# Two groups of operand sums behind the last plain column of three feed-forwards

## The chip, the cores and the metric

The kernel runs on one core of one Trainium2 chip, as one program. The metric is the device time of one execution in microseconds (us), the median over several runs. The engines named below are TensorE (PE, with its weight loads as PEld), VectorE (DVE), ScalarE (ACT), GpSimd (POOL) and SyncE (SP, which issues the loads of weights). Each engine goes through its own list of instructions in the order in which the program was laid out, and waits at an instruction until what it needs is there.

## The reference

An encoder trunk of two layers over 512 tokens of width 1024, in float32. Each layer has a feed-forward, a mixer, a second feed-forward and a gated embedding, so there are four feed-forwards in all.

```python
def swiglu(x, w_gu, w_down):
    g, u = jnp.split(x @ w_gu, 2, axis=-1)        # D_FF = 2816
    return (jax.nn.silu(g) * u) @ w_down

for i in range(DEPTH):                            # DEPTH = 2
    h = h + 0.5 * swiglu(rmsnorm(h, ffn1_norm[i]), ffn1_w_gu[i], ffn1_w_down[i])
    hn = rmsnorm(h, mix_norm[i])
    h = h + (ssd_mixer if i % 2 == 0 else neighbourhood_attention)(hn, ...)
    h = h + 0.5 * swiglu(rmsnorm(h, ffn2_norm[i]), ffn2_w_gu[i], ffn2_w_down[i])
    gate = jax.nn.sigmoid(rmsnorm(h, ple_norm[i]) @ ple_w_gate[i])
    h = h + gate * rmsnorm(p[i] @ ple_w_proj[i], ple_post_norm[i])
```

## The kernel before

Tokens lie along the free dimension (512 of them), features along the 128 partitions; `h` is eight tiles of 128x512. A product in float32 is made of three rounded ones: an operand is cut into a rounded part ("hi", or `wh` for weights) and the rest ("lo", `wl`), and `gemm` issues hi times hi (L298), hi times lo (L301) and lo times hi (L302) for each 128 rows of the inner dimension. ScalarE makes the rounded part of a weight tile (L231) and VectorE the rest (L233). There are three tiles of each, so the fourth weight can be cut only when the products with the first are through.

The 22 column blocks of a feed-forward's gate and up matrices are handled in two ways. The first ones are "plain": a gate product of 24 matmuls, an up product of 24 matmuls, then `activate` (L474 gate times the norm's factor, L475 silu, L477 and L478 the up half, L327 and L328 the cut into hi and lo). The others go two at a time through a scheme with seven smaller products per pair of columns (`block`, L539), which needs sums and differences of the residual's tiles. These are made once per feed-forward, in four groups, by `sums(kk)` for kk = 0 to 3: two scaled tiles (L498), differences (L501, L502, L520, L521) and their cuts (L507, L508, L327, L328, L524, L525). A group has 12 instructions on VectorE and six on ScalarE. It also may cut one weight tile ahead of its own work (`prep_next`).

The first feed-forward has six plain columns (`FIRST`), the other three have four (`OTHERS`, columns 0 to 3). In these three, the group 0 is called in column 1, the group 1 ahead of column 2, the group 2 ahead of column 3 and the group 3 behind column 3. After the plain columns come two "pairs" of down products: output tiles 0 and 1, then 2 and 3, each with four columns' results as the inner dimension, 12 matmuls per tile, 48 in all (called d0 to d3 below, each with its weight tile). Then the blocks begin.

`issue_after`, the tile pools and a list scheduler fix the order per engine: an instruction called earlier stands earlier unless the scheduler's own estimate has its input coming late. So where a call stands decides the place of its instructions on VectorE and ScalarE, and with them that of the weight cuts next to them. TensorE's list follows too: where the estimate has a weight late, products that come later in the program may be drawn ahead of it.

## Time and profile before

| | |
|---|---|
| median of 3 runs | 2274.69 us (2274.47 to 2274.8) |
| profiled execution | 2274.88 us |
| its span, first to last instruction | 2273.0 us |
| granted TensorE clock, mean | 0.999 |
| TensorE busy | 2265.7 us |
| VectorE busy | 1823.0 us |
| ScalarE busy | 1284.3 us |

The span is what the trace covers; the execution's time is 1.9 us longer. In a row of the timeline the first number is the start in us from the span's beginning, the second how long the row lasted; a row with x2 holds two instructions. A 128x512 matmul is listed with 0.39 us, but one starts every 0.227 us, because the next begins while the last results drain: the distance between starts shows whether TensorE waited. On VectorE too the listed time is longer than the distance between starts (0.68 us listed, 0.60 us from start to start for 128x512).

The last plain column and the pairs lie at 923 to 940 us in the second feed-forward, at 1322 to 1341 us in the third and at 1907 to 1924 us in the fourth.

### The profile page before, as it was taken

The page shows a single profiled execution, that of the slowest core. Times are in us where ns is not written, and L with a number is a line of the kernel's source. Part 1 is how long each engine was busy: PE and PEld are TensorE (multiplying, and loading weights), DVE is VectorE, ACT ScalarE, POOL GpSimd, SP SyncE. Part 2 cuts the span into 40 slices and gives each one's busy share as a digit, 9 for nine tenths or more (in the row PEclk, how much of TensorE's full clock was granted, in tenths as well). Part 3 has the DMA queues.
Part 4 walks back from the last instruction along what each step waited for, and adds up shares of the span by engine and source line. Part 5 has one row for each costly group of instructions (what it writes and reads, how often), then busy time and mean ns, then how long its engine had stood idle before and what let it go on. Part 6 is the DMA issues. An engine that isn't in the chain of part 4 may idle for free.

```text
span 2273.0 us, 33245 instructions
## 1 busy us (share of the span) xinstructions
PE 2265.7 (100%) x12458; PEld 1948.5 (86%) x12458; DVE 1823.0 (80%) x2711; ACT 1284.3 (57%) x2335; POOL 327.9 (14%) x261
## 2 busy tenths in 40 slices
PE   9999999999999999999999999999999999999999
PEld 7888888888888888888888888888888888988887
DVE  8788878988888958988885898888668758888866
ACT  6444445777677765544457555444557655544563
POOL 0000001345555651000003100000110010000020
PEclk9999999999999999999999999999999999999999
DMA  5323324444444643322323332332557732333232
GB/s 198 114 77 107 107 78 140 162 154 140 146 141 143 208 146 120 116 98 85 102 89 115 108 102 88 98 107 78 173 176 228 227 117 92 103 107 107 79 102 75
DMA packets 105089, 281.56 MB, mean 124 GB/s; under 512 B 13008, under 2 KB 13904, under 8 KB 104928
## 3 DMA queue, kind: packets, MB, share of 16 engines
q1 hardware_dynamic: 104640, 279.30, 37.8%
q8 instruction: 98, 1.61, 0.3%
q14 instruction: 63, 0.52, 0.1%
q10 hardware_dynamic: 288, 0.14, 0.0%
HBM read 259.70 MB, written 13.40 MB: 120 GB/s over the span
## 4 chain that ended last, share of the span: by engine, by line
PE 96%; DVE 3%; ACT 1%; issue 0%; DMA 0%; POOL 0%; SPq 0%; DVEq 0%; POOLq 0%
PE ps L539 31%; PE ps L298 19%; PE ps L302 19%; PE ps L301 19%; PE ps L1023 1%; PE ps L982 1%; PE ps L1377 1%; PE ps L1003 1%; PE ps L1431 1%; PE ps L938 1%; PE ps L927 1%; PE ps L1420 1%; DVE wl L233 0%; DVE md L328 0%; PE ps L1411 0%
## 5 line engine op out<-in xcount | busy, mean ns | idle before, releaser
L298 PE MATMUL ps<-md,wh 128*128 128x512 f32 (+1 forms) x2032 | 796.0, 392 | 0.9 <-ACT md L327 0.9
L302 PE MATMUL ps<-md,wl 128*128 128x512 f32 (+1 forms) x2032 | 790.5, 389 | 0.2 <-DVE wl L233 0.2
L301 PE MATMUL ps<-md,wh 128*128 128x512 f32 (+1 forms) x2032 | 790.1, 389 | 0.0
L231 ACT CAST wh<-wr 128x1024 fp32r<-128x1024 f32 (+2 forms) x395 | 351.7, 892 | 417.4 <-PE ps L301 200.3
L233 DVE TENSOR_TENSOR wl<-wr,wh 128x1024 fp32r<-128x1024 f32 (+2 forms) x395 | 417.6, 1058 | 97.4 <-ACT wh L231 91.6
L302 PEld LDWEIGHTS ps<-md,wl 128*128 128x128 f32 x2032 | 381.5, 188 | 82.3 <-DVE wl L233 1.5
L298 PEld LDWEIGHTS ps<-md,wh 128*128 128x128 f32 x2032 | 381.6, 188 | 77.8 <-ACT md L327 1.4
L301 PEld LDWEIGHTS ps<-md,wh 128*128 128x128 f32 x2032 | 382.0, 188 | 74.0 <-DVE md L598 0.5
L539 PE MATMUL ps<-md,wh 128*128 128x256 f32 (+1 forms) x1610 | 367.2, 308 | 0.0
L539 PE MATMUL ps<-sc,wh 128*128 128x512 f32 (+1 forms) x1190 | 362.3, 357 | 0.0
L364 POOL TENSOR_TENSOR sq<-sq,sq 128x512 f32<-128x512 f32 x71 | 100.9, 1422 | 1612.1 <-ACT sq L360 1261.7
L233 DVE TENSOR_TENSOR wl<-md,wh 128x1024 fp32r<-128x1024 f32 x175 | 214.0, 1223 | 113.6 <-ACT wh L231 112.8
L231 ACT CAST wh<-md 128x1024 fp32r<-128x1024 f32 x175 | 183.8, 1051 | 200.9 <-PE ps L539 129.0
L539 PEld LDWEIGHTS ps<-md,wh 128*128 128x128 f32 x1610 | 263.7, 190 | 20.3
L539 PE MATMUL ps<-md,wl 128*128 128x256 f32 x980 | 276.4, 282 | 0.0
L539 PE MATMUL ps<-sc,wl 128*128 128x256 f32 x980 | 275.7, 281 | 0.0
L539 PEld LDWEIGHTS ps<-sc,wh 128*128 128x128 f32 x1190 | 210.0, 188 | 34.6
L539 PEld LDWEIGHTS ps<-sc,wl 128*128 128x128 f32 x980 | 185.2, 189 | 3.2
L539 PEld LDWEIGHTS ps<-md,wl 128*128 128x128 f32 x980 | 186.1, 190 | 0.0
L827 DVE SCALAR_TENSOR_TENSOR t<-ps,ccw,t 128x510 f32<-128x510 f32 (+1 forms) x180 | 133.3, 743 | 10.5 <-ACT t L820 7.9
L629 DVE SCALAR_TENSOR_TENSOR hs<-ps,hs 128x512 f32<-128x512 f32 x144 | 98.7, 685 | 49.9 <-PE ps L302 49.6
L565 DVE TENSOR_TENSOR t<-ps,t 128x256 f32<-128x256 f32 x280 | 113.4, 417 | 14.0 <-ACT t L562 12.8
(214 smaller groups left out, 2446.4 us busy)
## 6 DMA issues: line engine op xcount, KB each, us to landing
wr<-in_w_gw_dram SPq DMA_DIRECT2D x70, 512.0 KB, 3.3
md<-in_w_gw_dram SPq DMA_DIRECT2D x70, 512.0 KB, 4.5
wr<-in_w_in_dram SPq DMA_DIRECT2D x65, 512.0 KB, 3.2
wr<-in_w_dn_dram SPq DMA_DIRECT2D x128, 256.0 KB, 2.6
wr<-in_w_gu_dram SPq DMA_DIRECT2D x32, 512.0 KB, 3.2
hs<-crow SPq DMA_DIRECT2D x64, 256.0 KB, 3.7
wr<-in_w_dn_dram SPq DMA_DIRECT2D x32, 384.0 KB, 3.1
wr<-in_w_qkv_dram SPq DMA_DIRECT2D x24, 512.0 KB, 4.0
```

The costliest lines, as they stand in the source:

```text
L231: splits.append(s.copy(out=hi[:, :n], in_=raw[:, :n]))
L233: split_raw.low = v.tensor_sub(out=lo[:, :n], in0=raw[:, :n], in1=hi[:, :n])
L298: m = te.matmul(out=pt, lhsT=hi[:, sl], rhs=part(xp, 0, cols), start=first and k == 0, stop=False)
L301: te.matmul(out=pt, lhsT=hi[:, sl], rhs=part(xp, 1, cols), start=False, stop=False)
L302: gemm.last = te.matmul(out=pt, lhsT=lo[:, sl], rhs=part(xp, 0, cols), start=False, stop=last and k == n - 1)
L364: (v if fast else g).tensor_add(out=self.acc, in0=self.acc, in1=q)
L539: mm = lambda o, w, x, st, sp_: te.matmul(out=o, lhsT=w, rhs=x, start=opens and st, stop=sp_, skip_group_check=not opens)
L565: whole.last = v.tensor_add(out=o, in0=pt[j][:, :HT], in1=o)
L629: v.scalar_tensor_tensor(out=h[d], in0=pt, scalar=0.5, in1=h[d], op0=ALU.mult, op1=ALU.add)
L827: v.scalar_tensor_tensor(out=a[:, lo:hi], in0=src[:, lo + o:hi + o], scalar=w(j), in1=a[:, lo:hi], op0=ALU.mult, op1=ALU.add)
L927: te.transpose(out=pt[:, cs(i)], in_=src[:, cs(c)], identity=ident)
L938: te.matmul(out=pt[:, cs(c)], lhsT=bt[:, dr, cs(c)], rhs=ct_[:, dr, cs(c)], start=True, stop=True)
```

## The change

Group 2 is no longer called ahead of column 3 in the three feed-forwards with four plain columns; it is called behind column 3, and then group 3. The first feed-forward keeps its order: behind its last column no group is left, and ahead of it the call stays.

```diff
             held.append((f, pg, pu))
             while held:
                 activate(*held.pop(0))
-            if left and f == chunks[0][1] - 1:
+            while left and f == chunks[0][1] - 1:
                 sums(left.pop(0))
...
             if what == "plain":
-                if left and R[0] is not None:
+                if left and R[0] is not None and (first or a[0] < chunks[0][1] - 1):
                     sums(left.pop(0))
                 gate_up(a[0])
```

No instruction is added or removed on any engine. GpSimd's list is the same, and SyncE's loads come in the same order. The numbers behind names are counters of the program and differ between the two kernels; the weight rests of d0 to d3 are `wl_8903`, `wl_8963`, `wl_9002`, `wl_9035` before and `wl_8905`, `wl_8935`, `wl_8974`, `wl_9035` in the change.

VectorE in the second feed-forward, from the last row of column 2's up half, before: `t_8991` and `t_8994` are column 3's gate and up, `t_8907` and `t_8909` the scaled tiles of group 2.

```order
L478 TENSOR_TENSOR t_8895<-t_8895,t_8892 128x512
L498 SCALAR_TENSOR_TENSOR t_8907<-hs_8371,cst,rt_8675 128x512
L498 SCALAR_TENSOR_TENSOR t_8909<-hs_8547,cst,rt_8675 128x512
L328 TENSOR_TENSOR md_8898<-t_8895,md_8898 128x512
L501 TENSOR_TENSOR t_8911<-t_8907 128x256
```

In the change, from the same row: `t_8963` and `t_8966` are column 3's gate and up, `t_8978` and `t_8980` the scaled tiles of group 2.

```order
L478 TENSOR_TENSOR t_8895<-t_8895,t_8892 128x512
L474 TENSOR_TENSOR t_8963<-ps_8901,rt_8675 128x512
L233 TENSOR_TENSOR wl_8935<-wr_8806,wh_8933 128x512
L328 TENSOR_TENSOR md_8898<-t_8895,md_8898 128x512
L477 TENSOR_TENSOR t_8966<-ps_8902,rt_8675 128x512
L233 TENSOR_TENSOR wl_8974<-wr_8866,wh_8972 128x512
L478 TENSOR_TENSOR t_8966<-t_8966,t_8963 128x512
L498 SCALAR_TENSOR_TENSOR t_8978<-hs_8371,cst,rt_8675 128x512
L498 SCALAR_TENSOR_TENSOR t_8980<-hs_8547,cst,rt_8675 128x512
L328 TENSOR_TENSOR md_8969<-t_8966,md_8969 128x512
```

What moved: the whole of group 2 now stands behind L477, the reading of column 3's up product, which it stood ahead of before.

VectorE at the rest of d3's weight (`wl_9035`), before: `t_9010` and `t_9011` belong to group 3, `wl_9071` is the rest of the first block's weight.

```order
L525 TENSOR_TENSOR md_9026<-t_9011,md_9026 128x256
L233 TENSOR_TENSOR wl_9035<-wr_8905,wh_9033 128x512
L525 TENSOR_TENSOR md_9021<-t_9010,md_9021 128x256
L525 TENSOR_TENSOR md_9026<-t_9011,md_9026 128x256
L233 TENSOR_TENSOR wl_9071<-wr_8610,wh_9069 128x1024
```

The same place in the change.

```order
L328 TENSOR_TENSOR md_9016<-t_9008,md_9016 128x512
L521 TENSOR_TENSOR t_9011<-t_9008,t_9010 128x256
L525 TENSOR_TENSOR md_9021<-t_9010,md_9021 128x256 x2
L525 TENSOR_TENSOR md_9026<-t_9011,md_9026 128x256 x2
L233 TENSOR_TENSOR wl_9035<-wr_8907,wh_9033 128x512
L233 TENSOR_TENSOR wl_9071<-wr_8610,wh_9069 128x1024
```

What moved: between L477 of column 3 and `wl_9035` stood group 3 without its last two instructions before; in the change both groups stand there in full.

TensorE at the first use of `wl_9035`, before: `ps_9067` and `ps_9068` are d2's and d3's sums, L539 is the first block.

```order
L302 MATMUL ps_9067<-md_8997,wl_9002 128x512
L302 MATMUL ps_9068<-md_8732,wl_9035 128x512
L298 MATMUL ps_9068<-md_8799,wh_9033 128x512
L301 MATMUL ps_9068<-md_8799,wh_9033 128x512
L302 MATMUL ps_9068<-md_8799,wl_9035 128x512
```

The same place in the change.

```order
L302 MATMUL ps_9067<-md_8969,wl_8974 128x512
L539 MATMUL ps_9105<-sc_8743,wh_9069 128x512
L539 MATMUL ps_9106<-sc_8743,wh_9069 128x512
L539 MATMUL ps_9137<-sc_8751,wh_9073 128x256 x2
L302 MATMUL ps_9068<-md_8732,wl_9035 128x512
L298 MATMUL ps_9068<-md_8799,wh_9033 128x512
```

What moved: four matmuls of the first two blocks, which use group 0 alone and no weight rest, are drawn ahead of the first use of `wl_9035`. As many matmuls of the pairs stand ahead of that use as before.

## The prediction

> **What bounds the kernel now.** I read the page first, then who waited for whom on TensorE, then the timeline at the last plain column and the pairs of the second, third and fourth feed-forward.

> ```profile
> PE 2265.7 (100%) x12458; PEld 1948.5 (86%) x12458; DVE 1823.0 (80%) x2711; ACT 1284.3 (57%) x2335; POOL 327.9 (14%) x261
> PE 96%; DVE 3%; ACT 1%; issue 0%; DMA 0%; POOL 0%; SPq 0%; DVEq 0%; POOLq 0%
> PE idle L132 <- DVE ones_d L124: 1.1, 1, 1.1
> PE ps L298 <- ACT md L327: 0.9, 1, 0.9
> ```

> TensorE is busy for the whole span and makes up 96% of the chain that ended last. Its two longest waits in the whole span are 1.1 us, at the program's start, and 0.9 us. So what delays TensorE lengthens the run by as much, and there is very little waiting to be won back. What the change moves is VectorE's, so the question is where VectorE is late for TensorE. First TensorE in the second feed-forward, at the ends of column 3's gate and up products, at the start of the pairs, and at the first use of d3's rest.

> ```profile
> 923.01 0.39 PE L302 MATMUL ps<-md,wl 128*128 128x512 f32 x1
> ...
> 928.45 0.39 PE L302 MATMUL ps<-md,wl 128*128 128x512 f32 x1
> 928.67 0.39 PE L298 MATMUL ps<-md,wh 128*128 128x512 f32 x1
> ...
> 936.86 0.39 PE L301 MATMUL ps<-md,wh 128*128 128x512 f32 x1
> 937.09 0.71 PE L302 MATMUL ps<-md,wl 128*128 128x512 f32 x2
> 937.64 0.39 PE L298 MATMUL ps<-md,wh 128*128 128x512 f32 x1
> ```

> The gate product ends at 923.01 + 0.39 = 923.40, the up product at 928.84. In the row with two L302 the second, at 937.09 + 0.23 = 937.32, is the first to use `wl_9035`. The two take 0.55 us to the next start instead of 0.45, so 0.10 us is lost there. VectorE at the same time:

> ```profile
> 922.53 0.68 DVE L478 TENSOR_TENSOR t<-t,t 128x512 f32<-128x512 f32 x1
> 923.13 1.40 DVE L498 SCALAR_TENSOR_TENSOR t<-hs,cst,rt 128x512 f32<-128x512 f32 x2
> ...
> 928.68 0.68 DVE L233 TENSOR_TENSOR wl<-wr,wh 128x512 fp32r<-128x512 f32 x1
> 929.28 0.68 DVE L474 TENSOR_TENSOR t<-ps,rt 128x512 f32<-128x512 f32 x1
> 929.89 0.68 DVE L477 TENSOR_TENSOR t<-ps,rt 128x512 f32<-128x512 f32 x1
> 930.48 0.68 DVE L233 TENSOR_TENSOR wl<-wr,wh 128x512 fp32r<-128x512 f32 x1
> 931.08 0.68 DVE L478 TENSOR_TENSOR t<-t,t 128x512 f32<-128x512 f32 x1
> 931.68 1.41 DVE L498 SCALAR_TENSOR_TENSOR t<-hs,cst,rt 128x512 f32<-128x512 f32 x2
> 933.01 0.68 DVE L328 TENSOR_TENSOR md<-t,md 128x512 fp32r<-128x512 f32 x1
> 933.61 0.42 DVE L501 TENSOR_TENSOR t<-t 128x256 f32<-128x256 f32 x1
> ...
> 936.56 0.68 DVE L233 TENSOR_TENSOR wl<-wr,wh 128x512 fp32r<-128x512 f32 x1
> 937.16 0.75 DVE L525 TENSOR_TENSOR md<-t,md 128x256 fp32r<-128x256 f32 x2
> 937.83 1.22 DVE L233 TENSOR_TENSOR wl<-wr,wh 128x1024 fp32r<-128x1024 f32 x1
> ```

> No row here carries a wait, and each starts where the one ahead of it leaves off: VectorE works without a pause through the whole column. It reads the up product at 929.89, 1.05 us after that is done, because group 2 (923.13 to 928.68) has filled the time until then. The rest of d3's weight (936.56 + 0.68 = 937.24) is ready 0.08 us before TensorE comes to it. So this place has no room left, and it is the one on which the forecast rests. Two casts of ScalarE give the time that a signal takes, and the second matters below:

> ```profile
> 931.80 0.62 ACT L327 CAST md<-t 128x512 fp32r<-128x512 f32 x1 [1.10 <-DVE t L478]
> ...
> 937.34 1.05 ACT L231 CAST wh<-md 128x1024 fp32r<-128x1024 f32 x1 [0.48 <-PE ps L301]
> ```

> The first starts 0.04 us after L478's end (931.08 + 0.68), the second 0.09 us after L301's (936.86 + 0.39). I take 0.07 us, an estimate between them.

> **The change part by part.** A group's price on VectorE comes from group 3: the two L498 take 933.01 - 931.68 = 1.33 us, L501 up to `wl_9035` 936.56 - 933.61 = 2.95, the last two L525 937.83 - 937.16 = 0.67, in sum 4.95 us. Group 2 agrees: 928.68 - 923.13 = 5.55, of which one L328, 0.60, is column 2's own.

> *Ahead of the up product's end* VectorE now has only L474 (from 923.40 + 0.07 = 923.47), one L233 and one L328, 0.60 each, to 925.27. Then L477 heads its list and waits for 928.84 + 0.07 = 928.91. That is 3.64 us in which VectorE does nothing, though group 2's inputs, the residual and the norm's factor, are there: it stands behind L477.

> *From then on* the list is L477, L233 of d2 and L478 (1.80 us, to 930.71), group 2 (4.95, to 935.66), column 3's L328 (0.60, to 936.26), group 3 (4.95, to 941.21), and `wl_9035` with 0.68 to 941.89, or 941.96 with the signal. Before, L477 to `wl_9035` took 937.24 - 929.89 = 7.35 us; now it takes 12.98, which is group 2 and the last two L525 more (4.95 + 0.67), and it begins 0.98 us earlier.

> *TensorE* would come to that place at 937.32, and has the four matmuls of the blocks drawn ahead: 2 x 0.23 + 2 x 0.12 = 0.69 us (the 0.12 is half the 0.23 of a matmul of twice the width). They are only moved, so they cost nothing of themselves and cover 0.69 us. It waits from 938.01 to 941.96: 3.95 us. The 0.10 us lost there before I count in both kernels. So the second feed-forward costs 3.95 us more.

> *What comes next* is not late. The first block's weight rest starts at 941.23 + 0.60 = 941.83 and is done by 943.05; TensorE needs it after d3's 10 other matmuls, at 941.96 + 10 x 0.227 = 944.23. Group 3 is done before `wl_9035`, and the blocks read it later still.

> *ScalarE and the queues.* ScalarE's cuts for both groups move with them. One cast of a block's weight stands among them, the L231 at 937.34. It waits for TensorE's last hi product of d2, which does not move, and takes some 0.95 us from start to start (an estimate: the listed 1.05 less 0.1, VectorE's listed time being 0.08 over its distance of starts). Group 3's last five casts stand behind it, from 938.29 on. VectorE comes to the first of their rests at about 938.95 by the sum above (L328 after 941.21 - 4 x 0.335 - 0.335 - 0.60), when its cast, 0.62 us long like the L327 above, has just ended at 938.91. So ScalarE costs nothing, with 0.0 us to spare; if it is late, VectorE is late by the same. It also means that the third and fourth of the drawn matmuls, which use this weight (ready at 938.39 + 0.07), wait inside the 3.95 us, not beside them. SyncE's order is unchanged and nothing on GpSimd moves, so I cost both at nothing; the cover of the loads is that d3's raw weight is needed no sooner than before.

> *The third feed-forward* differs: there VectorE is later, and TensorE waits now.

> ```profile
> 1327.63 0.39 PE L302 MATMUL ps<-md,wl 128*128 128x512 f32 x1
> 1327.86 0.39 PE L298 MATMUL ps<-md,wh 128*128 128x512 f32 x1
> ...
> 1330.13 0.39 PE L301 MATMUL ps<-md,wh 128*128 128x512 f32 x1
> 1330.67 0.50 PE L302 MATMUL ps<-md,wl 128*128 128x512 f32 x1 [0.16 <-DVE wl L233]
> 1331.01 0.40 PE L298 MATMUL ps<-md,wh 128*128 128x512 f32 x1
> ...
> 1332.40 0.39 PE L298 MATMUL ps<-md,wh 128*128 128x512 f32 x1
> 1333.72 0.73 PE L298 MATMUL ps<-md,wh 128*128 128x512 f32 x2 [0.93 <-ACT md L327]
> 1334.30 0.39 PE L301 MATMUL ps<-md,wh 128*128 128x512 f32 x1
> 1323.78 0.68 DVE L478 TENSOR_TENSOR t<-t,t 128x512 f32<-128x512 f32 x1
> 1331.14 0.68 DVE L477 TENSOR_TENSOR t<-ps,rt 128x512 f32<-128x512 f32 x1
> ```

> Lost against 0.23 us a start: 0.31 at 1330.13, 0.11 at 1330.67, 1.09 at 1332.40, 0.12 at 1333.72, in sum 1.63 us, because L477 is read 1331.14 - 1328.02 = 3.12 us late. The change removes these: after L478 at 1323.78 VectorE has four slots of 0.60 to 1326.18 and waits for 1328.02 too. The pair then runs as in the second feed-forward, counted from its start (1327.86 here, 928.67 there), and TensorE waits 3.95 us at d3. Net 3.95 - 1.63 = 2.3 us.

> *The fourth feed-forward* reads like the second, and I take 3.95 us again:

> ```profile
> 1912.61 0.39 PE L302 MATMUL ps<-md,wl 128*128 128x512 f32 x1
> ...
> 1921.25 0.72 PE L302 MATMUL ps<-md,wl 128*128 128x512 f32 x2
> 1921.81 0.40 PE L298 MATMUL ps<-md,wh 128*128 128x512 f32 x1
> ```

> From the up product's last row to that pair of L302 are 8.64 us, as in the second (937.09 - 928.45), with the same 0.1 us lost.

> **Sum.** 3.95 + 2.3 + 3.95 = 10.2 us. On the profiled execution: span 2273.0 + 10.2 = 2283.2, time 2274.88 + 10.2 = 2285.1; that execution is 0.19 us above the median, so the median becomes 2284.9 us, 0.45% slower. What is unknown is how near the sums of slots come: 12.98 us over some 30 instructions, with ScalarE just in time. Less than one slot of 0.60 too much gives 2283.1 for three places; a ScalarE that is late by one cast (0.62) at each gives 2286.8.

> **The rivals.**

> *The clock falls in the pause.* Between the drawn matmuls (the last starts at 938.46 + 0.12) and 941.96 TensorE rests some 3.3 us, three times in the run. No wait in the trace after the start is over 0.9 us, and the granted clock is 0.999 throughout, so the trace says nothing of a rest this long. If it halved the clock for as long as the rest itself, TensorE would lose half of 3.3 us each time: 3 x 1.65 = 5.0, so 2289.9. Against it: the rest is not complete, two matmuls stand a little ahead, and all is dense before and after. [...]

> *The wait is hidden (not slower).* If VectorE reached `wl_9035` by 938.01 there would be no wait at d3, and the third feed-forward would keep its gain: 2274.7 - 1.6 = 2273.1, 0.07% less. For this the 12.98 us from L477 would have to be 9.0, or a part of group 2 would have to run in VectorE's 3.64 us of rest. Against it: these slots are the same in all three feed-forwards, and L477 stands first.

> *ScalarE's late cast feeds back.* If the cast at 937.34 is itself later than now, group 3's last rests slip, then `wl_9035`, and with some 1 us at each place the run comes to 2287.9.

> **How the numbers follow.** 0.2% (4.5 us) is about what a measurement of this kernel can tell from no change. The forecast has 0.80 (own range 2283.1 to 2286.8), the falling clock 0.10, the feedback 0.04, the hidden wait 0.02; the 0.04 left is that each stall is only a third of what I take (some 3 us in all). Slower therefore 0.94, within 0.2% 0.05, faster 0.01. The range takes in the forecast's bounds and the clock: 2282.5 to 2290.

> **What would show it.** TensorE's list of waits should have a line for L302 on VectorE's L233 with three waits of about 3.3 us, and ScalarE's L231 or its weight for some 0.4 to 0.7 us before it. VectorE should rest about 3.6 us ahead of L477 in the second and fourth feed-forward, some 1.8 in the third, and the 0.9 us of L298 on L327 should be gone. Starts every 0.23 us behind the wait would mean that the clock held; 0.45 us that it fell. The forecast is wrong if L233 of d3 starts before 939 us.

## The result and the profile after

| | before | changed |
|---|---|---|
| median of 5 runs | 2274.8 us (2274.47 to 2275.22) | 2291.56 us (2290.88 to 2292.16) |
| ratio, 95% interval | | 1.0074 (1.0063 to 1.0085) |
| profiled execution | 2274.88 us | 2291.19 us |
| its span | 2273.0 us | 2289.1 us |
| mean granted clock | 0.999 | 0.997 |

The change makes the kernel 16.8 us slower. The forecast was 10.2 us slower, and the time lies 1.6 us above the range. The page, with the busy engines and the chain that ended last, shows little of where the 16.8 us are:

```profile
PE 2272.2 (99%) x12458; PEld 1953.3 (85%) x12458; DVE 1824.3 (80%) x2711; ACT 1283.7 (56%) x2335; POOL 328.0 (14%) x261
PE 96%; DVE 3%; ACT 1%; issue 0%; DMA 0%; POOL 0%; SPq 0%; POOLq 0%
```

TensorE is listed as busy 6.5 us longer with as many matmuls: some of them took longer. The list of what TensorE waited for (us in total, times, longest) has the other part:

```profile
PE ps L302 <- DVE wl L233: 9.1, 3, 3.0
PE ps L539 <- ACT wh L231: 1.5, 3, 0.5
```

These are the two waits that were forecast, at all three places. The 0.9 us of L298 on L327 is gone. TensorE's timeline in the second feed-forward, at the first use of d3's weight rest (`wl_9035`; below, "d3's rest" is always this tile, and an engine that does nothing is called idle):

```profile
936.82 0.39 PE L302 MATMUL ps<-md,wl 128*128 128x512 f32 x1
937.04 0.61 PE L539 MATMUL ps<-sc,wh 128*128 128x512 f32 x2
938.17 0.50 PE L539 MATMUL ps<-sc,wh 128*128 128x256 f32 x2 [0.51 <-ACT wh L231]
941.70 0.50 PE L302 MATMUL ps<-md,wl 128*128 128x512 f32 x1 [3.02 <-DVE wl L233]
942.03 0.39 PE L298 MATMUL ps<-md,wh 128*128 128x512 f32 x1
...
943.35 0.63 PE L302 MATMUL ps<-md,wl 128*128 128x512 f32 x1
943.77 0.63 PE L298 MATMUL ps<-md,wh 128*128 128x512 f32 x1
...
946.33 0.32 PE L539 MATMUL ps<-md,wl 128*128 128x256 f32 x1
946.49 0.40 PE L539 MATMUL ps<-md,wh 128*128 128x512 f32 x1
```

From the L302 at 936.82 to the one at 941.70 are 4.88 us. The L302 and the four drawn matmuls between need 3 x 0.227 + 2 x 0.114 = 0.91, so 3.97 us are lost, of which 0.10 was lost before: 3.87 us more. The same distance of 4.88 us stands in the third feed-forward (1341.60 to 1346.48) and in the fourth (1931.77 to 1936.65). Behind the wait starts are 0.23 us apart at first, but from 943 on 0.42 us, up to 946.4 (in the third and fourth feed-forward a slow stretch covers the first matmul behind the wait already). VectorE and ScalarE at the same place:

```profile
924.40 0.68 DVE L328 TENSOR_TENSOR md<-t,md 128x512 fp32r<-128x512 f32 x1
928.63 0.69 DVE L477 TENSOR_TENSOR t<-ps,rt 128x512 f32<-128x512 f32 x1 [3.55 <-PE ps L302]
...
939.61 1.43 DVE L525 TENSOR_TENSOR md<-t,md 128x256 fp32r<-128x256 f32 x4
940.96 1.82 DVE L233 TENSOR_TENSOR wl<-wr,wh 128x512 fp32r<-128x512 f32 x2
937.07 1.05 ACT L231 CAST wh<-md 128x1024 fp32r<-128x1024 f32 x1 [0.89 <-PE ps L301]
938.02 0.61 ACT L327 CAST md<-t 128x512 fp32r<-128x512 f32 x1
```

VectorE is idle for 3.55 us ahead of L477, and from L477 to TensorE's start with the rest are 941.70 - 928.63 = 13.07 us, against the 941.96 - 928.91 = 13.05 of the forecast. The cast on ScalarE ends at 938.12 and lets the third drawn matmul start.

The view by stretches gives the clock (columns: stretch, length, busy us and count of PE, PEld, DVE, ACT, POOL, then PEclk, DMA share and GB/s). The clock records of the trace are at half in 943.00 to 946.41, in 1345.77 to 1352.60 and in 1936.28 to 1939.69; the stretches are cut there:

```profile
936.17:939.58 3.41, 1.99 (x9) 1.21 (x7) 3.41 (x9) 2.50 (x6) 0.00 (x0) 1.00 0.00 0
939.58:943.00 3.42, 1.30 (x6) 1.09 (x7) 3.42 (x8) 0.41 (x1) 0.00 (x0) 1.00 0.11 29
943.00:946.41 3.41, 3.41 (x11) 2.73 (x10) 1.34 (x2) 1.04 (x1) 0.00 (x0) 0.50 0.80 268
946.41:949.82 3.41, 3.41 (x27) 3.23 (x26) 1.83 (x3) 1.69 (x3) 0.00 (x0) 1.00 0.04 16
1342.36:1345.77 3.41, 0.58 (x3) 0.30 (x2) 3.41 (x11) 2.38 (x6) 0.00 (x0) 1.00 0.00 0
1345.77:1349.18 3.41, 2.70 (x6) 2.16 (x7) 2.92 (x4) 0.00 (x0) 0.00 (x0) 0.50 0.51 161
1349.18:1352.60 3.42, 3.42 (x11) 2.82 (x10) 0.76 (x1) 1.04 (x1) 0.00 (x0) 0.50 0.43 146
1352.60:1356.01 3.41, 3.41 (x27) 3.24 (x26) 1.69 (x3) 1.69 (x3) 0.00 (x0) 1.00 0.00 0
1932.87:1936.28 3.41, 0.50 (x2) 0.30 (x2) 3.41 (x10) 2.05 (x6) 0.00 (x0) 1.00 0.00 0
1936.28:1939.69 3.41, 3.04 (x7) 2.48 (x8) 2.59 (x3) 0.00 (x0) 0.00 (x0) 0.50 0.64 173
```

The clock is at half for one, two and one stretches of 3.413 us. They lie on one grid: from 943.00 to 1345.77 are 402.77 us, 118 times 3.4133, and from there to 1936.28 are 590.51 us, 173 times. Below, a cell is one such piece of the grid. In the four slow cells TensorE was busy 3.41 + 2.70 + 3.42 + 3.04 = 12.57 us at a granted clock of 0.50, so 6.3 us are lost there by an estimate from that clock (by starts 0.426 us apart in place of 0.227, as from 1347.07 to 1350.48, it would be 5.9). With the 6.3 and the waits, 3 x 3.87 - 1.63 = 10.0 us, that makes 16.3 us, which is the difference of the two profiled executions (2291.19 - 2274.88).

### The profile page after: what moved, and what is told of

Same layout as the page of the kernel before. It is cut to its first block, busy times and chain, and to the rows that moved or that the text cites. A ratio compares the mean times of both kernels' runs of the same rounds, so it can differ in the third digit from the quotient of the medians.

```text
span 2289.1 us, 33236 instructions
## 1 busy us (share of the span) xinstructions
PE 2272.2 (99%) x12458; PEld 1953.3 (85%) x12458; DVE 1824.3 (80%) x2711; ACT 1283.7 (56%) x2335; POOL 328.0 (14%) x261
## 4 chain that ended last, share of the span: by engine, by line
PE 96%; DVE 3%; ACT 1%; issue 0%; DMA 0%; POOL 0%; SPq 0%; POOLq 0%
PE ps L539 30%; PE ps L302 20%; PE ps L298 19%; PE ps L301 19%; PE ps L1023 1%; PE ps L982 1%; PE ps L1377 1%; PE ps L1003 1%; PE ps L1431 1%; PE ps L938 1%; PE ps L927 1%; PE ps L1420 1%; DVE md L328 0%; DVE wl L233 0%; DVE t L498 0%
## 5 line engine op out<-in xcount | busy, mean ns | idle before, releaser
L302 PE MATMUL ps<-md,wl 128*128 128x512 f32 (+1 forms) x2032 | 793.3, 391 | 9.1 <-DVE wl L233 9.1
L298 PE MATMUL ps<-md,wh 128*128 128x512 f32 (+1 forms) x2032 | 798.2, 393 | 0.0
L301 PE MATMUL ps<-md,wh 128*128 128x512 f32 (+1 forms) x2032 | 791.6, 390 | 0.0
L231 ACT CAST wh<-wr 128x1024 fp32r<-128x1024 f32 (+2 forms) x395 | 351.7, 892 | 427.0 <-PE ps L301 210.1
L233 DVE TENSOR_TENSOR wl<-wr,wh 128x1024 fp32r<-128x1024 f32 (+2 forms) x395 | 417.9, 1060 | 97.4 <-ACT wh L231 91.4
L302 PEld LDWEIGHTS ps<-md,wl 128*128 128x128 f32 x2032 | 382.7, 188 | 91.7 <-DVE wl L233 10.6
L298 PEld LDWEIGHTS ps<-md,wh 128*128 128x128 f32 x2032 | 382.8, 188 | 76.5 <-ACT wh L231 0.4
L301 PEld LDWEIGHTS ps<-md,wh 128*128 128x128 f32 x2032 | 382.8, 188 | 74.1 <-DVE md L598 0.4
L539 PE MATMUL ps<-md,wh 128*128 128x256 f32 (+1 forms) x1610 | 367.7, 308 | 0.0
L539 PE MATMUL ps<-sc,wh 128*128 128x512 f32 (+1 forms) x1190 | 363.0, 357 | 1.5 <-ACT wh L231 1.5
L233 DVE TENSOR_TENSOR wl<-md,wh 128x1024 fp32r<-128x1024 f32 x175 | 214.1, 1224 | 115.8 <-ACT wh L231 115.0
L231 ACT CAST wh<-md 128x1024 fp32r<-128x1024 f32 x175 | 183.8, 1051 | 212.1 <-PE ps L539 127.6
L539 PEld LDWEIGHTS ps<-md,wh 128*128 128x128 f32 x1610 | 264.1, 190 | 20.7
L539 PE MATMUL ps<-md,wl 128*128 128x256 f32 x980 | 276.6, 282 | 0.0
L539 PE MATMUL ps<-sc,wl 128*128 128x256 f32 x980 | 276.3, 282 | 0.0
L539 PEld LDWEIGHTS ps<-sc,wh 128*128 128x128 f32 x1190 | 210.2, 189 | 37.2 <-ACT wh L231 2.8
L539 PEld LDWEIGHTS ps<-sc,wl 128*128 128x128 f32 x980 | 185.8, 190 | 3.6
L539 PEld LDWEIGHTS ps<-md,wl 128*128 128x128 f32 x980 | 186.4, 190 | 0.0
```

The source lines that it names most:

```text
L231: splits.append(s.copy(out=hi[:, :n], in_=raw[:, :n]))
L233: split_raw.low = v.tensor_sub(out=lo[:, :n], in0=raw[:, :n], in1=hi[:, :n])
L298: m = te.matmul(out=pt, lhsT=hi[:, sl], rhs=part(xp, 0, cols), start=first and k == 0, stop=False)
L301: te.matmul(out=pt, lhsT=hi[:, sl], rhs=part(xp, 1, cols), start=False, stop=False)
L302: gemm.last = te.matmul(out=pt, lhsT=lo[:, sl], rhs=part(xp, 0, cols), start=False, stop=last and k == n - 1)
L539: mm = lambda o, w, x, st, sp_: te.matmul(out=o, lhsT=w, rhs=x, start=opens and st, stop=sp_, skip_group_check=not opens)
```

## The experiments

The theory: some 10 us of the 16.8 are waits for d3's rest, behind which two whole groups now stand on VectorE, and some 6.3 us are the clock, which falls because TensorE is idle in those waits. The rivals: the idle time does not make the clock fall and the 6.5 us come from elsewhere; it is VectorE's own idle time ahead of L477 that costs; the move of group 3 costs as much as that of group 2. All times are medians, of 5 runs or of 11; the kernel before, run beside them, had 2274.84 us (first four kernels) and 2274.58 us (last three).

**Twelve fillers.** This fills the pause with matmuls whose result nobody reads. No instruction of VectorE is added. The edit also calls d2's and d3's products one after the other and not side by side; on TensorE the first two of d3 then stand behind the last three of d2, where the changed kernel had them ahead.

```diff
-            te.matmul(out=pt, lhsT=hi[:, sl], rhs=part(xp, 1, cols), start=False, stop=False)
...
+            m = te.matmul(out=pt, lhsT=hi[:, sl], rhs=part(xp, 1, cols), start=False, stop=False)
+            if fill and k == 0:
+                spare_ = px_bank()
+                with tc.issue_after(m.ins):
+                    for _ in range(fill[0]):
+                        m = te.matmul(out=spare_, lhsT=mean[1.0], rhs=fill[1], start=True, stop=True)
...
-                    side_by_side(pts, mine)
+                    if first or not d:
+                        side_by_side(pts, mine)
+                    else:
+                        ws = [unit() for _ in pts]
+                        gemm(pts[0], ws[0], mine)
+                        gemm(pts[1], ws[1], mine, fill=(12, xs[0][0]))
```

> The changed kernel with twelve matmuls of 128x512 added on TensorE in the pause of each of the three feed-forwards, between d2's products and the four drawn block matmuls; their result goes to a spare bank and is read by nobody. VectorE and ScalarE work as in the changed kernel. Twelve starts at 0.227 us are 2.7 us, so of some 3.8 us of waiting about 1.1 us are left at each place. Theory (the rest of TensorE makes the clock fall): the fall goes, the waits stay as long in sum, so 2291.6 less some 6.5 us, 2285, with starts of 0.227 us behind the wait and a clock of 0.999. Rival (the time beyond the waits comes from elsewhere, on VectorE or ScalarE): the fillers change nothing, 2291 to 2292. Second rival (the time at the pause is not free, the fillers push the products back): 36 x 0.227 = 8.2 us more, 2299.

Measured: 2285.22 us (2284.44 to 2285.76), ratio 1.0045 (1.0032 to 1.0057); the granted clock is 1.00 in each of nine stretches around the three pauses, and 1.000 as the run's mean. TensorE's list of waits (the lines added move L302 to L308 and L539 to L545):

```profile
PE ps L308 <- DVE wl L233: 3.0, 3, 1.0
```

Its timeline in the second feed-forward:

```profile
936.82 2.95 PE L306 MATMUL ps<-sc,mean 128*128 128x512 f32 x12
939.62 0.85 PE L545 MATMUL ps<-sc,wh 128*128 128x512 f32 x4
941.45 0.50 PE L308 MATMUL ps<-md,wl 128*128 128x512 f32 x1 [0.98 <-DVE wl L233]
941.79 0.40 PE L298 MATMUL ps<-md,wh 128*128 128x512 f32 x1
```

36 matmuls more make the kernel 6.3 us faster than the changed one. TensorE starts with d3's rest 0.25 us earlier (941.45 against 941.70), but VectorE's reading of the up product already starts 0.23 us earlier (928.40 against 928.63), and from there to d3's rest VectorE takes 12.31 us here (to 940.71) and 12.33 in the changed kernel (to 940.96). So the delay by VectorE is the same, and the 10.4 us that are left over the kernel before are its price without the clock. The forecast had 10.2.

**Four fillers.** The same with 4 in place of 12.

> The same with four filler matmuls at each place, 0.9 us, so that the rest which is left is 2.1 to 2.9 us instead of 3.0 with 0.5 ahead of it. If the fall needs a rest of about the 3.4 us that one slow stretch of the changed kernel lasts: no fall, 2285 as with twelve. If any rest of 2 us does it, or a share of one: falls at all three places, 2291 to 2292. If it is a matter of where the rest lies against a window that runs on freely: falls at some of the three places, 1.7 us each, 2286 to 2290.

Measured: 2289.75 us (2286.53 to 2291.28), ratio 1.0062 (1.0049 to 1.0074). Each wait for the rest is 2.85 us, and the clock falls at all three places, once each. Its second place:

```profile
1341.23:1344.64 3.41, 2.54 (x13) 1.91 (x11) 3.41 (x10) 2.60 (x6) 0.00 (x0) 1.00 0.00 0
1344.64:1348.06 3.42, 1.45 (x6) 1.23 (x7) 3.42 (x7) 0.48 (x2) 0.00 (x0) 1.00 0.14 36
1348.06:1351.47 3.41, 3.41 (x11) 2.76 (x11) 1.46 (x2) 1.04 (x1) 0.00 (x0) 0.50 0.77 265
```

A single wait shorter than a cell is enough, then: the slow cell stands behind one in which TensorE was busy for 1.45 us of 3.42. Behind the cell with 2.54 the clock stayed. The profiled run by itself, with three falls, is the second case that was expected. But the five runs are 4.8 us apart, and the mean granted clock of each goes with its time: 0.999 in the two of 2286.53 and 2286.88 us, 0.998 or 0.997 in the three of 2289.75 us and more. That fits the third case (where the idle time lies against a grid that runs on by itself); only the profiled run shows its cells.

**The third feed-forward alone.**

```diff
-                if left and R[0] is not None and (first or a[0] < chunks[0][1] - 1):
+                if left and R[0] is not None and (first or between or a[0] < chunks[0][1] - 1):
```

> The change in the third feed-forward alone; the second and the fourth as before. Theory: 3.84 us of waits less the 1.63 us that stand there before, 2.2 us, and one or two slow stretches of 1.7 us each: 2274.8 + 3.9 to 5.6 = 2278.7 to 2280.4. If the clock plays no part: 2277.0. If the three places cost the same without the 1.63: a third of 16.8, 2280.4.

Measured: 2278.96 us (2278.52 to 2279.96), ratio 1.0018 (1.0009 to 1.0027), 4.1 us more. TensorE's timeline at d3's rest:

```profile
1340.99 0.50 PE L302 MATMUL ps<-md,wl 128*128 128x512 f32 x1 [3.02 <-DVE wl L233]
```

And its stretches on the grid:

```profile
1338.78:1342.19 3.41, 1.20 (x5) 1.00 (x6) 3.41 (x8) 0.48 (x2) 0.00 (x0) 1.00 0.08 11
1342.19:1345.61 3.42, 3.42 (x11) 2.72 (x10) 1.22 (x2) 1.04 (x1) 0.00 (x0) 0.50 0.79 283
```

The wait is the same, and here one slow cell follows where the changed kernel has two. 3.87 - 1.63 + 3.42 / 2 = 3.95 us, as measured within 0.2. A third of 16.8 (5.6 us) is not what it costs.

**Group 3 behind the pairs too.** Group 2 stays where the change put it.

```diff
-            while left and f == chunks[0][1] - 1:
+            if left and f == chunks[0][1] - 1:
                 sums(left.pop(0))
...
                     owed += [(d, pts[0]), (d + 1, pts[1])]
+                    while left and d:
+                        sums(left.pop(0))
```

> Group 2 behind column 3 as in the changed kernel, so VectorE still rests 3.6 us ahead of the up product's reading; group 3 is called behind the second pair, so that d3's weight rest comes ahead of its last part on VectorE. Theory (what costs is the five microseconds of the second group ahead of d3's rest, not VectorE's own rest): the wait of 3 us at d3 goes, a later wait of 0.5 to 1.5 us at the first blocks at each place, no fall of the clock, less the 1.63 us of the third feed-forward: 2274 to 2279. Rival (the 3.6 us that VectorE loses ahead of the up product must come back somewhere on TensorE, whatever the order): 3 x 3.64 = 10.9 less 1.6, 2284 or, with the clock, 2290.

Measured: 2278.14 us (2277.18 to 2278.73), ratio 1.0015 (1.0006 to 1.0024); no slow cell (granted clock 1.00 in each of nine stretches around the three places). VectorE's timeline in the second feed-forward:

```profile
928.87 0.69 DVE L477 TENSOR_TENSOR t<-ps,rt 128x512 f32<-128x512 f32 x1 [3.55 <-PE ps L302]
...
935.22 0.69 DVE L233 TENSOR_TENSOR wl<-wr,wh 128x512 fp32r<-128x512 f32 x1
```

TensorE's list of waits:

```profile
PE ps L539 <- ACT wh L231: 1.1, 3, 0.4
PE ps L539 <- DVE wl L233: 0.9, 3, 0.3
PE ps L539 <- DVE md L525: 0.8, 3, 0.3
```

VectorE is idle for the same 3.55 us ahead of L477. But d3's rest is cut at 935.22 with group 3 behind it, so TensorE finds it ready and waits only later, at the blocks, 2.8 us in all as listed. By the distance of starts TensorE loses some 1.4 us to these waits at each place, 4.3 in all; less some 1.7 us that the third feed-forward gains, that is 2.6 of the 3.1 us by which the profiled spans differ (2276.1 against 2273.0), and the other 0.5 us are not accounted for. So VectorE's idle time as such does not cost 10 us; it costs what is due before VectorE has caught up.

**Group 3 alone behind the pairs.** Group 2 stands ahead of column 3 as in the kernel before.

```diff
-            if left and f == chunks[0][1] - 1:
+            if first and left and f == chunks[0][1] - 1:
                 sums(left.pop(0))
...
+                    while left and d:
+                        sums(left.pop(0))
```

> The other half of the pair of moves: group 2 stays ahead of column 3 as before, group 3 alone goes behind the second pair. VectorE then cuts d3's rest ahead of group 3. Theory (d3's rest is late only where two whole groups stand between the up product's reading and it): no wait at d3; the 1.63 us of the third feed-forward stay; the blocks' weights may be late by some 0.3 us a place: 2274.8 to 2275.8. Rival (moving group 3 behind the pairs costs as much by itself as with group 2 moved too, 3.3 us, and the 1.6 us that the other won in the third feed-forward): 2279.7.

Measured: 2274.66 us (2274.42 to 2275.21), ratio 1.0001 (0.9992 to 1.0009): no difference. Group 3 did not go behind d3's rest as a whole: the scheduler drew about half of it ahead, and VectorE cuts d3's rest at 935.22 between its L328 and its L520, 1.34 us earlier than before (936.56). The wait of the third feed-forward stays as it was:

```profile
PE ps L298 <- ACT md L327: 0.9, 1, 0.9
PE ps L302 <- DVE wl L233: 0.2, 1, 0.2
```

Over the kernel before, the four orders cost 0 (neither group moved), 0.1 (group 3 behind the pairs), 3.3 (group 2 behind column 3, group 3 behind the pairs) and 16.8 us (group 2 behind column 3, group 3 where it was). None of them is faster than the kernel before.

**Ten and seven fillers.** These test what makes the clock fall: the work in a cell, or the length of the wait. The shares of a cell in the next text are not counted by the listed busy time; by that, the cells with a fall behind them held 0.50 to 1.45 us (15 to 42 per cent), and the two emptiest of these three kernels with full clock behind them 1.99 and 2.09 us (58 and 61 per cent).

> Ten fillers at each place, so that about 1.5 us of rest are left. In the traces of the changed kernel, of four fillers and of the change in the third feed-forward alone, the half-clock stretches begin and end on a grid of 3.413 us that runs through the whole execution, and each falls on a cell behind one in which TensorE was at work for 10 to 42 per cent; cells of 48 and 51 per cent were followed by full clock. Theory (a cell's share of work decides, the limit near 43 per cent, so 1.95 us of rest in one cell): 1.5 us never do it, no fall, 2285.2 as with twelve, the runs no further apart than there. Rival (any rest of over about 1 us can do it, or the length of a single wait decides with a limit between 1.0 and 3.0): some falls, 2286 to 2290.

Measured with ten: 2285.26 us (2285.07 to 2286.16), ratio 1.0048 (1.0036 to 1.0061), no slow cell (granted clock 1.0 in the profiled run). Each wait is 1.4 us. The emptiest of its cells:

```profile
1929.55:1932.96 3.41, 1.97 (x10) 1.50 (x9) 3.41 (x8) 0.81 (x2) 0.00 (x0) 1.00 0.00 0
```

> Seven fillers, about 2.2 us of rest left. Theory (share of work in a cell, limit near 43 per cent): a fall only where 1.95 us of the rest lie in one cell, which a rest of 2.2 us meets in about half of the positions; so one or two falls of 1.7 us in a run, 2285 to 2289, median about 2287.5, runs apart by multiples of about 1.7. Each fall must follow a cell with less than 0.45 of work. Rival (the length of the wait alone decides): no fall in all runs, 2285.2, or three in all runs, 2290.

Measured with seven: 2287.39 us (2284.5 to 2288.15), ratio 1.0055 (1.0041 to 1.0068). The three waits are of one length, 2.14 or 2.15 us, and the clock falls behind one of them:

```profile
939.12:942.53 3.41, 1.27 (x7) 0.94 (x6) 3.41 (x8) 0.81 (x2) 0.00 (x0) 1.00 0.00 0
942.53:945.94 3.41, 3.41 (x10) 2.66 (x10) 1.47 (x2) 0.48 (x1) 0.00 (x0) 0.50 0.78 258
1345.30:1348.71 3.41, 2.17 (x9) 1.80 (x10) 3.41 (x5) 0.02 (x1) 0.00 (x0) 1.00 0.34 97
1348.71:1352.12 3.41, 3.41 (x23) 3.07 (x22) 1.61 (x3) 2.12 (x3) 0.00 (x0) 1.00 0.60 210
1932.40:1935.81 3.41, 1.90 (x8) 1.60 (x9) 3.41 (x6) 0.29 (x1) 0.00 (x0) 1.00 0.24 64
1935.81:1939.22 3.41, 3.41 (x22) 3.02 (x22) 1.88 (x3) 1.85 (x3) 0.00 (x0) 1.00 0.77 249
```

Equal waits, and unlike ends: the wait's length alone does not decide. The cell with the fall behind it held 1.27 us of work, the emptiest at the other two places 2.17 and 1.90 us. In the pauses of all kernels here, each cell at full clock in which TensorE was busy for 1.45 us or less (eight of them) was followed by a slow one, and none with 1.90 us or more was. The granted clock of the runs, 1.0 in the one of 2284.5 us and 0.999 in the other four, fits a fastest run without a fall.

## Why the prediction was wrong

**The waits were right.** At each place 3.87 us were forecast as 3.95; VectorE's idle times of 3.55, 1.59 and 3.55 us as 3.64, 1.8 and 3.64; the wait for ScalarE's cast, 0.51 us, as 0.4 to 0.7. The third feed-forward kept its gain: matmuls that start 5.35 us later than before ahead of its pairs (1331.85 against 1326.50) start 3.64 us later within them (1340.91 against 1337.27), a gain of 1.71 us where 1.63 was forecast. The sum of these, forecast as 10.2 us, is 10.0 us in the trace, and 10.4 and 10.7 us in the kernels with twelve and with ten fillers, where the clock stayed at full.

**The step that failed is the choice against the falling clock.** That rival had 0.10; it is what happened. "Against it: the rest is not complete, two matmuls stand a little ahead, and all is dense before and after" was no argument: the cell ahead of the first fall held 1.30 us of busy TensorE and the clock fell all the same. Nor was it so that "the trace says nothing of a rest this long": the kernel before shows a fall at its own end. Its last matmul there ends at 2268.44, and the clock is at half from 2270.38 on, behind a cell with 1.47 us of work and under 2 us without any. These are the last whole cell of its grid and what follows:

```profile
2266.97:2270.38 3.41, 1.47 (x13) 1.26 (x11) 2.12 (x5) 0.42 (x2) 0.00 (x0) 1.00 0.13 47
2270.38:2273.00 2.62, 0.00 (x0) 0.00 (x0) 0.00 (x0) 0.00 (x0) 0.00 (x0) 0.50 0.14 50
```

The mean of 0.999 over the span hides it. My 0.10 for the rival rested on no run, and the idle time that I forecast, 3.3 us, is almost one cell long (3.41 us). The cells ahead of the falls were not empty either: they held 0.50 to 1.45 us of busy TensorE in the pauses, and 1.47 us at that end.

**The rival's price was too small as well.** I let the clock fall "for as long as the rest itself", 1.65 us a place and 5.0 in all. No run shows that. The changed kernel shows it at half for a whole cell of 3.41 us, and in the third feed-forward for a second one: four cells, 12.57 us of busy time, 6.3 us by the estimate above. The range ended 0.1 us above that price, so the rival's own size had no room in it.

**The other rivals.** The wait was not hidden. ScalarE's late cast did not feed back: from L477 to TensorE's start came to 13.07 us.

## What to carry to other kernels

An engine that gets its work one step later is idle now and late afterwards; look for the next thing that is due behind the moved work in its list, and ask whether that thing could be cut ahead of it. Where a wait of over some 2 us on TensorE is forecast, add the clock to its price: in these runs a wait of 2.1 to 3.0 us was followed by one 3.4 us cell at a granted clock of 0.50, at times by two, and at times by none (2.14 and 2.15 us, at two places of three); waits of 1.4 us by none. With ten or twelve matmuls without use in each pause the clock stayed at full; with four it fell at all three places of the profiled run. A rival whose price is an estimate should be priced on both sides of it, and the range should hold its price and not end there.

## What the runs showed of the hardware

```profile
2270.62:2274.03 3.41, 1.68 (x15) 1.48 (x13) 2.02 (x5) 0.65 (x2) 0.00 (x0) 1.00 0.20 74
2274.03:2276.87 2.84, 0.00 (x0) 0.00 (x0) 0.10 (x1) 0.00 (x0) 0.00 (x0) 1.00 0.13 46
```

Of all these cells, the fullest with a slow one behind it held 1.47 us and the emptiest with full clock behind it 1.68 us, one cell each. In slow cells the changed kernel shows 2.70 us of work followed by a second slow cell, and 3.04 us followed by full clock; one such pair shows no more than that. The five runs with seven fillers are 3.7 us apart and those with ten 1.1 us. Counted in cells of 3.4133 us from the span's start, the slow pieces begin 0.9 us into a cell in the profiled run of the changed kernel, 3.2 with four fillers and 0.5 with seven, so the grid's place differed between these runs. That it differs also between the runs of one kernel would explain how far they are apart, and their granted clocks go that way, but it was not shown: the cells of the runs that weren't profiled are not known.
